# A hybrid decoder layer on one core: where the products of each group of heads stand, and which engine copies the state

## The chip, the cores and the metric

The kernel runs on one core of a Trainium2 chip. A core has a tensor engine (PE, matmuls and transposes; PEld is its weight load), a vector engine (DVE), a scalar engine (ACT), GpSimd (POOL) and a queue engine for transfers (SP). Each takes its instructions in a fixed order, and they wait for one another by semaphores. The metric is the time of one execution of the program on the device, in microseconds (us); of several runs the median is taken. One further execution is recorded by the hardware profiler; all durations below come from it.

## The reference

One decoder layer, `SEQ` 256, `D_MODEL` 2048, in float32:

```python
u = rmsnorm(h, norm_mix_pre)
z, xbc, dt_raw, q, k, v = split(u @ w_in)
xbc = silu(causal_depthwise_conv(xbc, conv_w, conv_b))     # width 4
xs, bm, cm = split(xbc)                                    # 8 groups of 4 heads, state 128
a_cs = cumsum(dt * a)                                      # chunks of 128: two of them
decay_in = exp(where(causal, a_cs[i] - a_cs[j], -inf))
y_diag = (cb * decay_in) @ xdt                             # within a chunk
states = bm^T (decay_to_end * xdt)                         # state at the end of a chunk
y_off = (cc @ previous_state) * exp(a_cs)                  # read-out of the earlier chunk
yg = (y_diag + y_off + d_skip * xh) * silu(z)
y_ssm = grouped_rmsnorm(yg) * ssm_norm_w
y_att = dilated_window_attention(q, k, v)                  # three dilations, mixed
h = h + rmsnorm(concat(y_ssm, y_att) @ w_out, norm_mix_post)
h = h + rmsnorm(relu(rmsnorm(h) @ w_up) ** 2 @ w_down, norm_mlp_post)
```

The change lies in the groups of heads: `y_diag`, `states` and `y_off` for each of the eight groups.

## The kernel before, in words

Most of the time goes to the large products with the weights `w_in`, `w_out`, `w_up` and `w_down` in columns of 512. Weights come from memory in blocks of two rows of 128 (`raw`, 512 KB). Each block is split in two: ScalarE writes the high part (`hi`, L147) and VectorE the rest (`lo`, L148). PE multiplies with both (L475 with `hi`, L478 with `lo` where a product has its features on the partitions; L328 to L330 and L411 to L413 where it has the positions there). A product over all 2048 rows is eight blocks, and a block of the first kind is eight L475 and eight L478. There are five buffers each for `hi` and `lo` and four for `raw`, so ScalarE's split of a later block waits until PE has finished with an earlier one.

The smaller work is written as Python generators, which are laid in between. A deque `waiting` holds them. After each block of weights `pump()` takes the first generator, runs it up to its next `yield` (one portion) and puts it at the deque's end. With two groups of heads in the deque, a group advances by one portion every second block. The groups come in pairs: two are queued after the conv of each set of x columns, and are laid into the blocks of the products that follow. In the trace these are the places near 140 to 160 us (groups 0 and 1), 186 to 207 us (2 and 3), 292 to 310 us (4 and 5) and 330 to 352 us (6 and 7). After groups 0 to 3 and 4 to 7 the gate columns and then further columns of `w_in` follow.

A group's generator (`ssd_group`) has these portions. First the cumulated decays are fetched into `bc` (L787). Then L793 to L811: C times B (`cbm`), B and x turned round by transposes, and on VectorE and GpSimd the scaled x (`xdt`, `xdd`, `xs`). Then the decays: `Relu` and `Exp` on ScalarE (L820, L821), times `cbm` on VectorE (L822); the state's product (L825, into one half of a small bank `ps`) and its copy `st` (L827). Then the read-out with the state (L829, into the other half of the same bank), its scaling by VectorE (`yo`, L831), its sum on GpSimd (L833), and eight products of the decays with `xdt` (L837) in a new bank. VectorE adds and gates (L840, L842), ScalarE squares (L846), VectorE and GpSimd work out the root (L141, L142), VectorE scales (L850). After two empty portions the result is turned round (L857) and split into `sh` and `sl` (L149, L150) for the product with `w_out`.

All small work shares two banks (`psmall`), which go round: a bank can be taken again when its last reader is done. `Exp` (L821) and `Silu` (L753, L776) need different tables in ScalarE; before a change of table an `ACT_TABLE_LOAD` stands in its order.

A scheduler sets the final order of instructions on each engine from the order in which they were written, from priorities (`tc.high_priority`; the weights' fetches and splits have the highest, `AHEAD`) and from what each depends on. So a moved portion can shift other instructions too.

Of the kernel before, what the change touches and what calls it, by code (L numbers as in the profile page):

```python
# [13 lines left out]
AF = mybir.ActivationFunctionType  # L14
# [3 lines left out]
S = 256  # L18
# [59 lines left out]
def hymba_layer(ctx: ExitStack, tc: tile.TileContext, x, norm_mix_pre, w_in, conv_w, conv_b, dt_bias, a_log,  # L78
                d_skip, ssm_norm_w, w_out, norm_mix_post, norm_mlp_pre, w_up, w_down, norm_mlp_post,
                consts, out):  # L80
    nc = tc.nc
# [53 lines left out]
    def psmall():  # L135
        return psm.tile([P, NB], F32, name="ps")

    def rsqrt_mean(dst, sums, n):

        m = cp.tile(list(sums.shape), F32, name="rm", bufs=2)  # L140
        nc.vector.tensor_scalar(m, sums, 1.0 / n, EPS, op0=ALU.mult, op1=ALU.add)  # L141
        nc.gpsimd.tensor_tensor(dst, m, half[:, :sums.shape[1]], op=ALU.pow)  # L142

    def split(hi, lo, src, scale=None):

        if scale is None:
            return (nc.scalar.activation(hi, src, AF.Copy),  # L147
                    nc.vector.tensor_tensor(lo, src, hi.bitcast(F32), op=ALU.subtract))  # L148
        return (nc.scalar.activation(hi, src, AF.Copy, scale=scale),  # L149
                nc.vector.scalar_tensor_tensor(lo, src, scale, hi.bitcast(F32), op0=ALU.mult, op1=ALU.subtract))  # L150
# [632 lines left out]
    def ssd_group(sp, g, bT, cT, xT, z):  # L783

        hs = slice(HPG * g, HPG * (g + 1))
        bc = sp.tile([P, HPG, S], F32, name="bc")
        nc.scalar.dma_start(bc, acs_d[hs].partition_broadcast(P))  # L787
        yield

        p = psmall()  # L790
        for c in range(NT):
            cs = slice(c * P, (c + 1) * P)
            nc.tensor.matmul(p[:, cs], bT[:, cs], cT[:, cs], start=True, stop=True)  # L793
        nc.tensor.transpose(p[:, S:S + P], bT[:, 0:P], ident)
        cbm = sp.tile([P, NT, P], F32, name="cbm")
        nc.vector.tensor_tensor(cbm, p[:, :S].rearrange("p (c i) -> p c i", c=NT),
                                triu[:, None, :].to_broadcast([P, NT, P]), op=ALU.mult)
        bn = sp.tile([P, P], F32, name="bn")
        nc.scalar.activation(bn, p[:, S:S + P], AF.Copy)

        p = psmall().rearrange("p (c f) -> p c f", c=NT)
        for c in range(NT):
            for f in range(2):
                nc.tensor.transpose(p[:, c, f * P:(f + 1) * P], xT[:, f, c * P:(c + 1) * P], ident)
        xs = sp.tile([P, NT, HPG, HD], F32, name="xs")
        nc.scalar.activation(xs.rearrange("p c r d -> p c (r d)"), p, AF.Copy)
        xdt = sp.tile([P, NT, HPG, HD], F32, name="xdt")
        for c in range(NT):
            nc.vector.tensor_tensor(xdt[:, c], xs[:, c], dt[:, c, hs, None].to_broadcast([P, HPG, HD]), op=ALU.mult)
        xdd = sp.tile([P, HPG, HD], F32, name="xdd")  # L810
        nc.gpsimd.tensor_tensor(xdd, xdt[:, 0], toend[:, hs, None].to_broadcast([P, HPG, HD]), op=ALU.mult)  # L811
        for c in range(NT):
            nc.gpsimd.tensor_tensor(xs[:, c], xs[:, c], skip_b[:, hs, None].to_broadcast([P, HPG, HD]), op=ALU.mult)
        yield

        for c in range(NT):
            m = bc[:, :, c * P:(c + 1) * P]
            for r in range(HPG):
                h = HPG * g + r
                nc.scalar.activation(m[:, r], m[:, r], AF.Relu, scale=-1.0, bias=acs[:, c, h:h + 1])  # L820
            nc.scalar.activation(m, m, AF.Exp, scale=-1.0)  # L821
            nc.vector.tensor_tensor(m, m, cbm[:, c, None, :].to_broadcast([P, HPG, P]), op=ALU.mult)  # L822

        p = psmall()
        nc.tensor.matmul(p[:, :S], bn, xdd.rearrange("p r d -> p (r d)"), start=True, stop=True)  # L825
        st = sp.tile([P, HPG * HD], F32, name="st")
        nc.vector.tensor_copy(st, p[:, :S])  # L827
        yield
        nc.tensor.matmul(p[:, S:], cT[:, P:], st, start=True, stop=True)  # L829
        yo = sp.tile([P, HPG, HD], F32, name="yo")  # L830
        nc.vector.tensor_tensor(yo, p[:, S:].rearrange("p (r d) -> p r d", r=HPG),  # L831
                                eacs[:, hs, None].to_broadcast([P, HPG, HD]), op=ALU.mult)
        nc.gpsimd.tensor_tensor(xs[:, 1], xs[:, 1], yo, op=ALU.add)  # L833
        p = psmall().rearrange("p (c r d) -> p c r d", c=NT, r=HPG)
        for c in range(NT):
            for r in range(HPG):
                nc.tensor.matmul(p[:, c, r], bc[:, r, c * P:(c + 1) * P], xdt[:, c, r], start=True, stop=True)  # L837

        yg = sp.tile([P, NT, HPG * HD], F32, name="yg")
        nc.vector.tensor_tensor(yg, p.rearrange("p c r d -> p c (r d)"), xs.rearrange("p c r d -> p c (r d)"),  # L840
                                op=ALU.add)
        nc.vector.tensor_tensor(yg, yg, z, op=ALU.mult)  # L842
        gs = sp.tile([P, NT], F32, name="gs")
        for c in range(NT):
            junk = sp.tile([P, HPG * HD], BF16, name="gj")
            nc.scalar.activation(junk, yg[:, c], AF.Square, accum_out=gs[:, c:c + 1])  # L846
        gr = sp.tile([P, NT], F32, name="gr")
        rsqrt_mean(gr, gs, HPG * HD)
        for c in range(NT):
            nc.vector.tensor_scalar(yg[:, c], yg[:, c], gr[:, c:c + 1], None, op0=ALU.mult)  # L850
        yield
        yield
        yield
        p = psmall().rearrange("p (f s) -> p f s", f=2)
        for f in range(2):
            for c in range(NT):
                nc.tensor.transpose(p[:, f, c * P:(c + 1) * P], yg[:, c, f * P:(f + 1) * P], ident)  # L857
        with tc.high_priority(offset=200):
            for f in range(2):
                k = 2 * g + f  # L860
                split(sh[:, k], sl[:, k], p[:, f], w_ssm[:, k:k + 1])
# [3 lines left out]
    for hb in range(2):  # L865
        bT = conv_block(COL_B + hb * NB, 16 + 4 * hb, first if hb == 0 else None)
        if hb == 0:
            waiting.append(steps())
        cT = conv_block(COL_C + hb * NB, 24 + 4 * hb)
        for xb in (2 * hb, 2 * hb + 1):  # L870
            xT = conv_block(COL_X + xb * NB, 4 * xb)
            if xb % 2 == 0:
                zs += gates(xb)
            for j in range(2):
                g = 2 * xb + j
                waiting.append(ssd_group(sp, g, bT[:, g % 4], cT[:, g % 4], xT[:, 2 * j:2 * j + 2],
                                         zs[xb][:, :, j * 256:(j + 1) * 256]))
# [623 lines left out]
```

## Time and profile before

| | us |
|---|---|
| median of three runs | 1458.86 (1458.23 to 1462.82) |
| the profiled execution's own time | 1459.04 |
| its span, first to last instruction | 1457.3 |
| PE busy in it | 1446.1 (99%) |
| weight loads of PE | 1219.4 (84%) |
| DVE busy | 1281.2 (88%) |
| ACT busy | 939.1 (64%) |
| POOL busy | 150.3 (10%) |

The granted clock of TensorE was 0.999 of full speed. A row of a timeline gives the start and the duration in us, the engine, the line, the operation with the tile it writes and those it reads, and in brackets the engine's idle time ahead of it with what ended it. A row that has `x8` stands for eight in a run, and its duration is that of the whole run. A row of groups gives the total busy time and the mean in ns, and behind the second bar the idle time ahead of them. A row of stretches gives for each engine the busy time and, in brackets, the number of instructions; then the clock, the share of the DMA engines and GB/s.

### The profile page before, as it was taken

To read this page: it belongs to the slowest core of one execution; us is meant where nothing else is said; L and a number is where in the kernel's file an instruction comes from. 1 tells how busy PE (TensorE), PEld (TensorE's weight loads), DVE (VectorE), ACT (ScalarE), POOL (GpSimd) and SP (SyncE) were. 2 spreads that over 40 slices of the span, in tenths; PEclk is the share of its full clock that TensorE was granted. 3 is DMA by queue.
4 is the path that set the end of the run, shared out by engine and by line. 5 is a ranking of instruction groups with operands and counts; after the bars stand their busy time and mean duration, and the time that the engine had idled before them with its cause. 6 is when DMAs were issued, how large, how long until landed. Compare 5 with 4: busy or idle time off the path is not lost.

```text
span 1457.3 us, 20381 instructions
## 1 busy us (share of the span) xinstructions
PE 1446.1 (99%) x7099; PEld 1219.4 (84%) x7099; DVE 1281.2 (88%) x1843; ACT 939.1 (64%) x1346; POOL 150.3 (10%) x226
## 2 busy tenths in 40 slices
PE   9999999999999999999999999999999999999998
PEld 8888888888888888888888888888888888888886
DVE  7799898888997686689878999999889999999997
ACT  7577779566666565556657677656464776765664
POOL 0202120121010010010100011011111111101000
PEclk9999999999999999999999999999999999999999
DMA  8978556856675486688876798678888888788854
GB/s 271 279 204 235 177 175 185 247 174 202 186 220 174 130 238 202 194 261 253 270 224 213 207 318 240 196 223 255 249 238 275 257 245 247 208 281 258 260 181 160
DMA packets 170201, 328.27 MB, mean 225 GB/s; under 512 B 15617, under 2 KB 18545, under 8 KB 170097
## 3 DMA queue, kind: packets, MB, share of 16 engines
q1 hardware_dynamic: 144592, 272.37, 58.6%
q0 software_dynamic: 17632, 40.91, 14.0%
q10 hardware_dynamic: 7872, 13.68, 2.7%
q8 instruction: 56, 0.92, 0.2%
q14 instruction: 49, 0.39, 0.1%
HBM read 322.67 MB, written 45.12 MB: 252 GB/s over the span
## 4 chain that ended last, share of the span: by engine, by line
PE 95%; DVE 3%; ACT 1%; issue 1%; POOL 0%; ACTq 0%; DVEq 0%
PE acc L475 13%; PE acc L328 11%; PE acc L330 11%; PE acc L329 11%; PE acc L478 7%; PE acc L412 6%; PE acc L413 6%; PE acc L411 6%; PE ps L330 3%; PE ps L328 3%; PE ps L329 3%; PE ps L412 3%; PE ps L413 2%; PE ps L411 2%; DVE lo L148 1%; PE ps L837 1%
## 5 line engine op out<-in xcount | busy, mean ns | idle before, releaser
L148 DVE TENSOR_TENSOR lo<-raw,hi 128x1024 fp32r<-128x1024 f32 (+1 forms) x392 | 476.8, 1221 | 86.0 <-ACT hi L147 82.7
L147 ACT ACTIVATE hi<-raw 128x1024 fp32r<-128x1024 f32 (+1 forms) x392 | 409.7, 1050 | 209.0 <-PE acc L330 70.6
L475 PE MATMUL acc<-ua,hi 128*128 128x512 f32 x600 | 162.5, 400 | 0.0
L475 PEld LDWEIGHTS acc<-ua,hi 128*128 128x128 f32 x600 | 105.5, 189 | 16.4
L147 ACT ACTIVATE hi<-e 128x1024 fp32r<-128x1024 f32 x64 | 68.1, 1064 | 69.1 <-DVE e L252 64.2
L478 PEld LDWEIGHTS acc<-ua,lo 128*128 128x128 f32 x600 | 88.2, 190 | 10.0
L478 PE MATMUL acc<-ua,lo 128*128 128x256 f32 x600 | 91.5, 282 | 0.0
L328 PE MATMUL acc<-hi,sh 128*128 128x512 f32 x224 | 88.4, 395 | 0.0
L330 PE MATMUL acc<-hi,sl 128*128 128x512 f32 x224 | 87.3, 390 | 0.0
L329 PE MATMUL acc<-lo,sh 128*128 128x512 f32 x224 | 87.2, 389 | 0.0
L328 PE MATMUL acc<-hi,ua 128*128 128x512 f32 x216 | 85.5, 396 | 0.0
L329 PE MATMUL acc<-lo,ua 128*128 128x512 f32 x216 | 84.2, 390 | 0.0
L330 PE MATMUL acc<-hi,ua 128*128 128x512 f32 x216 | 84.2, 390 | 0.0
L148 DVE TENSOR_TENSOR lo<-e,hi 128x1024 fp32r<-128x1024 f32 x64 | 78.0, 1219 | 0.0
L475 PE MATMUL acc<-uc,hi 128*128 128x512 f32 x240 | 69.9, 402 | 0.0
L412 PE MATMUL acc<-lo,ah 128*128 128x512 f32 x174 | 67.8, 390 | 0.0
L411 PE MATMUL acc<-hi,ah 128*128 128x512 f32 x174 | 67.8, 389 | 0.0
L413 PE MATMUL acc<-hi,al 128*128 128x512 f32 x174 | 67.7, 389 | 0.0
L148 DVE TENSOR_TENSOR lo<-ha,hi 128x1024 fp32r<-128x1024 f32 x43 | 52.3, 1221 | 5.9 <-ACT hi L147 5.7
L147 ACT ACTIVATE hi<-ha 128x1024 fp32r<-128x1024 f32 x43 | 45.1, 1056 | 16.2 <-PE acc L330 9.5
L147 ACT ACTIVATE hi<-r 128x512 fp32r<-128x512 f32 x64 | 40.1, 627 | 18.3 <-PE acc L330 7.0
L330 PE MATMUL acc<-hi,al 128*128 128x512 f32 x128 | 49.8, 389 | 0.0
(544 smaller groups left out, 3612.7 us busy)
## 6 DMA issues: line engine op xcount, KB each, us to landing
raw<-in_w_in_dram SPq DMA_DIRECT2D x161, 512.0 KB, 4.5
raw<-in_w_down_dram SPq DMA_DIRECT2D x72, 512.0 KB, 5.2
raw<-in_w_up_dram SPq DMA_DIRECT2D x65, 512.0 KB, 4.7
raw<-in_w_out_dram SPq DMA_DIRECT2D x38, 512.0 KB, 5.1
pair<-in_w_up_dram POOLq DMA_DIRECT2D x56, 256.0 KB, 5.0
raw<-pair SPq DMA_DIRECT2D x52, 256.0 KB, 4.2
pair<-in_w_down_dram POOLq DMA_DIRECT2D x50, 256.0 KB, 6.2
ha<-in_w_up_dram SPq DMA_DIRECT2D x20, 512.0 KB, 4.9
```

Of the source, the lines that this page charges most:

```text
L147: return (nc.scalar.activation(hi, src, AF.Copy), nc.vector.tensor_tensor(lo, src, hi.bitcast(F32), op=ALU.subtract))
L148: nc.vector.tensor_tensor(lo, src, hi.bitcast(F32), op=ALU.subtract))
L328: nc.tensor.matmul(dst, a_h[:, r, ts], hi[:, j], start=begin and j == 0, stop=False)
L329: nc.tensor.matmul(dst, a_h[:, r, ts], lo[:, j], start=False, stop=False)
L330: product[t] = nc.tensor.matmul(dst, a_l[:, r, ts], hi[:, j], start=False, stop=end and j == KB - 1)
L411: nc.tensor.matmul(dst, a_h, hi[:, j], start=own and first, stop=False)
L412: nc.tensor.matmul(dst, a_h, lo[:, j], start=False, stop=False)
L413: nc.tensor.matmul(dst, a_l, hi[:, j], start=False, stop=own and last)
L475: nc.tensor.matmul(acc[f], hi[:, j, f * P:(f + 1) * P], u(k0 + j), start=k0 + j == 0, stop=False, skip_group_check=True)
L478: nc.tensor.matmul(acc[f][:, 0], lo[:, j, f * P:(f + 1) * P], u(k0 + j)[:, 0], start=False, stop=k0 + j == NK - 1, skip_group_check=True)
L837: nc.tensor.matmul(p[:, c, r], bc[:, r, c * P:(c + 1) * P], xdt[:, c, r], start=True, stop=True)
```

## The change

Three edits in `ssd_group`. The copy of the state from its bank goes from VectorE to ScalarE. A `yield` is put between the read-out's part (up to L833) and the decays' products (before L837, now L838), so these become a portion of their own with what follows them (L840 to L850, now L841 to L851). One of the two empty portions ahead of the transposes is taken out (of three `yield`s in a row two are left), so the number of portions of a group stays the same.

```diff
         p = psmall()
         nc.tensor.matmul(p[:, :S], bn, xdd.rearrange("p r d -> p (r d)"), start=True, stop=True)
         st = sp.tile([P, HPG * HD], F32, name="st")
-        nc.vector.tensor_copy(st, p[:, :S])
+        nc.scalar.activation(st, p[:, :S], AF.Copy)
         yield
         nc.tensor.matmul(p[:, S:], cT[:, P:], st, start=True, stop=True)
         yo = sp.tile([P, HPG, HD], F32, name="yo")
         nc.vector.tensor_tensor(yo, p[:, S:].rearrange("p (r d) -> p r d", r=HPG),
                                 eacs[:, hs, None].to_broadcast([P, HPG, HD]), op=ALU.mult)
         nc.gpsimd.tensor_tensor(xs[:, 1], xs[:, 1], yo, op=ALU.add)
+        yield
         p = psmall().rearrange("p (c r d) -> p c r d", c=NT, r=HPG)
...
             nc.vector.tensor_scalar(yg[:, c], yg[:, c], gr[:, c:c + 1], None, op0=ALU.mult)
-        yield
         yield
         yield
         p = psmall().rearrange("p (f s) -> p f s", f=2)
```

How the order of the instructions moves is shown at three places. First PE at groups 0 and 1: `st` is the state, `xdt` the scaled x, `bc` the decays, `uc`, `ua`, `hi` and `lo` belong to the blocks of weights. Before:

```order
L829 MATMUL ps<-st,cT 128x256
L475 MATMUL acc<-uc,hi 128x512 x2
L478 MATMUL acc<-uc,lo 128x256 x2
L475 MATMUL acc<-uc,hi 128x512 x2
L478 MATMUL acc<-uc,lo 128x256 x2
L837 MATMUL ps<-xdt,bc 128x64 x8
L475 MATMUL acc<-uc,hi 128x512 x2
L478 MATMUL acc<-uc,lo 128x256 x2
L475 MATMUL acc<-uc,hi 128x512 x2
L478 MATMUL acc<-uc,lo 128x256 x2
L829 MATMUL ps<-st,cT 128x256
L837 MATMUL ps<-xdt,bc 128x64 x8
```

After, from the second L829 (group 1) on; the eight rows of weights between it and the first L829 (group 0) are the same, without L837 among them:

```order
L829 MATMUL ps<-st,cT 128x256
L475 MATMUL acc<-ua,hi 128x512 x2
L478 MATMUL acc<-ua,lo 128x256 x2
L475 MATMUL acc<-ua,hi 128x512 x2
L478 MATMUL acc<-ua,lo 128x256 x2
L475 MATMUL acc<-ua,hi 128x512 x2
L478 MATMUL acc<-ua,lo 128x256 x2
L475 MATMUL acc<-ua,hi 128x512 x2
L478 MATMUL acc<-ua,lo 128x256 x2
L838 MATMUL ps<-xdt,bc 128x64 x8
L475 MATMUL acc<-ua,hi 128x512 x8
L478 MATMUL acc<-ua,lo 128x256 x8
```

Group 0's products, which stood half a block after its read-out, now stand two blocks after it, and group 1's, which followed its read-out at once, also two (a further L838 x8 follows the last row).

Second, VectorE ahead of group 2's state, up to the first split `sl` (L150) of an earlier group's result out of its bank (`cbm` is C times B, `xdt` the scaled x, `cT` and `pad` are columns of the next x, `lo` a block of weights). Before, from behind the first `cbm` (L796) and the two L822 on:

```order
L499 TENSOR_TENSOR cT<-acc,cT 128x256
L148 TENSOR_TENSOR lo<-raw,hi 128x1024
L499 TENSOR_TENSOR cT<-acc,cT 128x256 x2
L809 TENSOR_TENSOR xdt<-xs,dt 128x256
L148 TENSOR_TENSOR lo<-raw,hi 128x1024
L499 TENSOR_TENSOR cT<-acc,cT 128x256
L809 TENSOR_TENSOR xdt<-xs,dt 128x256
L796 TENSOR_TENSOR cbm<-ps,cst 128x256
L809 TENSOR_TENSOR xdt<-xs,dt 128x256 x2
L744 TENSOR_TENSOR pad<-cT,rbc 128x2x256 x2
L148 TENSOR_TENSOR lo<-raw,hi 128x1024
L150 SCALAR_TENSOR_TENSOR sl<-ps,par,sh 128x256
```

After, from behind the first `cbm` on:

```order
L809 TENSOR_TENSOR xdt<-xs,dt 128x256
L499 TENSOR_TENSOR cT<-acc,cT 128x256
L809 TENSOR_TENSOR xdt<-xs,dt 128x256
L499 TENSOR_TENSOR cT<-acc,cT 128x256
L822 TENSOR_TENSOR bc<-bc,cbm 128x4x128
L499 TENSOR_TENSOR cT<-acc,cT 128x256 x2
L796 TENSOR_TENSOR cbm<-ps,cst 128x256
L148 TENSOR_TENSOR lo<-raw,hi 128x1024
L809 TENSOR_TENSOR xdt<-xs,dt 128x256 x2
L744 TENSOR_TENSOR pad<-cT,rbc 128x2x256 x2
L822 TENSOR_TENSOR bc<-bc,cbm 128x4x128
L148 TENSOR_TENSOR lo<-raw,hi 128x1024
```

The L150 follows there too. The same work stands in both but for the splits of weights: three L148 before, two now; the third has gone ahead of the first `cbm`. Behind this L150 stand two L751, one L148 and two more L150 before, and three L751, one L148 and two more L150 now.

Third, PE at groups 6 and 7, where L825 makes the state. Before, from group 7's L825 on:

```order
L825 MATMUL ps<-xdd,bn 128x256
L475 MATMUL acc<-ua,hi 128x512
L829 MATMUL ps<-st,cT 128x256
L475 MATMUL acc<-ua,hi 128x512 x7
L478 MATMUL acc<-ua,lo 128x256 x6
L829 MATMUL ps<-st,cT 128x256
L478 MATMUL acc<-ua,lo 128x256 x2
L475 MATMUL acc<-ua,hi 128x512 x8
L478 MATMUL acc<-ua,lo 128x256 x2
L837 MATMUL ps<-xdt,bc 128x64 x16
```

After, from group 6's read-out L829 on; its L825 stands five rows higher, with four L475 and four L478 in between:

```order
L829 MATMUL ps<-st,cT 128x256
L475 MATMUL acc<-ua,hi 128x512 x6
L825 MATMUL ps<-xdd,bn 128x256
L475 MATMUL acc<-ua,hi 128x512 x2
L478 MATMUL acc<-ua,lo 128x256 x8
L838 MATMUL ps<-xdt,bc 128x64 x8
L475 MATMUL acc<-ua,hi 128x512
L829 MATMUL ps<-st,cT 128x256
L475 MATMUL acc<-ua,hi 128x512 x7
L478 MATMUL acc<-ua,lo 128x256 x8
L838 MATMUL ps<-xdt,bc 128x64 x8
```

Both states were made before either was read; now group 6 is read first, and group 7's state is made after that. In the built program both states now go to the same one of the two small banks, so group 7's L825 comes behind group 6's L831. From the last products to the transposes L857 stood six L478 and two blocks, and now two blocks.

At the same place, ScalarE after the change (`cT` are copies of finished columns, `sh` the split of an earlier group's result, `bc` the decays, `hi` a block of weights):

```order
L820 ACTIVATE bc<-bc,acs 128x128 x2
L827 ACTIVATE st<-ps 128x256
L820 ACTIVATE bc<-bc,acs 128x128 x3
L147 ACTIVATE hi<-raw 128x1024
L149 ACTIVATE sh<-ps,par 128x256
L821 ACTIVATE bc<-bc 128x4x128
L820 ACTIVATE bc<-bc,acs 128x128 x3
L147 ACTIVATE hi<-raw 128x1024
L821 ACTIVATE bc<-bc 128x4x128
L827 ACTIVATE st<-ps 128x256
```

The two L827 are new in this order; the second stands behind a split and an `Exp`. The tables move as well: ScalarE has as many `ACT_TABLE_LOAD` as before, but two that stood ahead of groups 2 and 3 (for an `Exp`, L821, between two `Silu`, L753) now stand behind them, at the gate columns near 212 to 265 us.

## The prediction

> **What bounds the kernel now.** I read the page's totals first, then the chain that ended last, and then the waits of the tensor engine alone, since these say how much any change off that engine can give back.
>
> ```profile
> PE 1446.1 (99%) x7099; PEld 1219.4 (84%) x7099; DVE 1281.2 (88%) x1843; ACT 939.1 (64%) x1346; POOL 150.3 (10%) x226
> PE 95%; DVE 3%; ACT 1%; issue 1%; POOL 0%; ACTq 0%; DVEq 0%
> ```
>
> PE is the bound: busy 99% of the span, and 95% of the chain. The change alters no matmul, so what can be won is PE's idle time. The list of its waits has eight rows (what PE waited for; total, times, longest). Four are outside the groups of heads:
>
> ```profile
> PE ps L1353 <- ACT dg L1352: 1.7, 1, 1.7
> PE ps L526 <- DVE half L515: 1.1, 1, 1.1
> ...
> PE acc L1131 <- DVE ha L1122: 0.2, 1, 0.2
> PE ps L412 <- DVE lo L148: 0.2, 1, 0.2
> ```
>
> The other four lie in the code that the change touches. The timeline of PE gives their places and sizes:
>
> ```profile
> 150.76 1.44 PE L837 MATMUL ps<-xdt,bc 128*128 128x64 f32 x11 [0.73 <-DVE yo L831]
> ...
> 191.77 0.67 PE L825 MATMUL ps<-xdd,bn 128*128 128x256 f32 x2 [1.76 <-DVE sl L150]
> ...
> 198.63 0.70 PE L829 MATMUL ps<-st,cT 128*128 128x256 f32 x2 [0.17 <-DVE st L827]
> ...
> 321.79 0.86 PE L475 MATMUL acc<-ub,hi 128*128 128x512 f32 x3
> 323.13 0.71 PE L793 MATMUL ps<-cT 128*128 128x128 f32 x4 [0.49 <-ACT bn L799]
> ```
>
> 0.73 + 1.76 + 0.17 + 0.49 = 3.15 us, or 0.22% of the span. That is the ceiling of the gain, and it lies below 0.3% (4.4 us), which is about what a measurement of this kernel can tell from no change. A loss has no such ceiling. So the question is which of the four waits go, and which come in their place. I number the pairs of groups 1 to 4 (groups 0/1 near 140 to 160 us, 2/3 near 186 to 207, 4/5 near 292 to 310, 6/7 near 330 to 352).
>
> The profiled execution took 1459.04 us with a span of 1457.3; it stands 0.18 above the median of the runs, 1458.86.
>
> **The products get their own portion: pair 1.** Before, one portion holds the read-out L829, its scaling L831 on VectorE and the products L837. PE reaches L837 of group 0 while L831 is still queued on VectorE, and both tiles go through the same two small banks: that is the 0.73. Now two blocks of weights stand between the read-out and the products, where half a block or none stood (first place of the order above). A block takes about 2.8 us (the two L829 quoted under pair 4, at 336.37 and 339.18, have 7 of its 8 L475 and 6 of its 8 L478 between them). L831 was 0.73 late for L837, so with 1.5 blocks (4.2 us) more it is 3.5 early: gain 0.73. The other bank's user comes a block later too, and the number of portions up to the transposes is the same, so I put no new wait here; a bound for one is the same 0.73.
>
> **The copy on ScalarE: pairs 1 and 3.** What it takes away and what it adds, and the nearest prices:
>
> ```profile
> L827 DVE COPY st<-ps x8: 410/412/423, 146.8 to 338.7; 128x256 f32<-128x256 f32 x8
> ...
> L498 ACT ACTIVATE cT<-acc 128x256 f32<-128x256 f32 x56 | 21.0, 381 | 16.4 <-PE acc L478 16.2
> L147 ACT ACTIVATE hi<-raw 128x1024 fp32r<-128x1024 f32 (+1 forms) x392 | 409.7, 1050 | 209.0 <-PE acc L330 70.6 <-PE acc L475 49.3 <-issue 21.1
> ```
>
> VectorE loses 8 x 0.412 = 3.3 us over four pairs; ScalarE gains 8 x 0.38 = 3.0 us (L498 has the same shape, source and operation, so I take it). Neither is PE's time. In pair 1 the copy falls into ScalarE's idle time:
>
> ```profile
> 147.32 1.06 ACT L147 ACTIVATE hi<-raw 128x1024 fp32r<-128x1024 f32 x1 [2.16 <-PE acc L475]
> ```
>
> ```profile
> 144.80 0.59 PE L825 MATMUL ps<-xdd,bn 128*128 128x256 f32 x2
> ```
>
> ```profile
> 146.76 0.41 DVE L827 COPY st<-ps 128x256 f32<-128x256 f32 x1
> ...
> 148.83 0.41 DVE L827 COPY st<-ps 128x256 f32<-128x256 f32 x1
> ```
>
> ScalarE idles 2.16 us because it waits for PE to free a buffer. The matmul L825 of group 1 stands at 144.80, so its copy can be done by about 146, where VectorE began it only at 148.83. Cost nothing; the cover is the 2.16, and were it gone, the split behind the copy would be 0.38 late. Pair 3 had no wait of PE, and its copies stand between the same splits. Between 0 and 0.38 for each of the four I take 0.
>
> **Pair 2.** The 1.76 is a wait for a bank: L825 of group 2 needs the second half of the split L150 out of it. VectorE's rows up to there:
>
> ```profile
> 176.57 0.42 DVE L796 TENSOR_TENSOR cbm<-ps,cst 128x256 f32<-128x256 f32 x1 [0.63 <-PE ps L794]
> ...
> 178.12 0.69 DVE L822 TENSOR_TENSOR bc<-bc,cbm 128x512 f32<-128x512 f32 x1 [0.40 <-ACT bc L821]
> 179.34 0.42 DVE L499 TENSOR_TENSOR cT<-acc,cT 128x256 f32<-128x256 f32 x1 [0.53 <-ACT cT L498]
> ...
> 189.23 0.87 DVE L751 SCALAR_TENSOR_TENSOR cT<-pad,cw,cT 128x256 f32<-128x256 f32 x2
> 190.02 1.21 DVE L148 TENSOR_TENSOR lo<-raw,hi 128x1024 fp32r<-128x1024 f32 x1
> 191.15 0.86 DVE L150 SCALAR_TENSOR_TENSOR sl<-ps,par,sh 128x256 fp32r<-128x256 f32 x2
> ```
>
> The run starts at 176.57 on a PE event and has no idle after the 0.53. In the changed order (second place above) one lo split (1.22) less stands in that run and one L751 (0.43) more: 0.79 less. The two small idles, 0.40 and 0.53, are behind ScalarE, which now has two table loads fewer ahead of this place: up to 0.93 more. So L150 comes 0.79 to 1.72 earlier against PE, and 0.04 to 0.97 of the 1.76 is left. I take 0.3 left, since ScalarE loses 2 x 1.28 us of loads there (rows below), more than the 0.93: gain 1.46, between 0.79 and 1.72. Further on, the copies of groups 2 and 3 stand behind one table load with its SiLU on ScalarE and are due at L829, 6.9 us after L825 of the same group (191.77 and 198.63): the 0.17 goes.
>
> **The table loads that move.** The groups' loads are as many as before, but two come to stand in the stretch 212 to 265 us, where the gates' columns run:
>
> ```profile
> 176.16 1.28 ACT L821 ACT_TABLE_LOAD   x1
> 177.46 0.64 ACT L821 ACTIVATE bc<-bc 128x512 f32<-128x512 f32 x1
> ```
>
> ```profile
> 220.00:240.00 20.00, 20.00 (x114) 17.42 (x113) 15.89 (x26) 19.88 (x36) 1.57 (x3) 1.00 0.66 185
> ```
>
> ```profile
> 247.58 2.36 DVE L148 TENSOR_TENSOR lo<-raw,hi 128x1024 fp32r<-128x1024 f32 x2
> ```
>
> ```profile
> 250.60 0.39 PE L328 MATMUL acc<-hi,ua 128*128 128x512 f32 x1
> 250.83 0.39 PE L329 MATMUL acc<-lo,ua 128*128 128x512 f32 x1
> ```
>
> ScalarE is busy 19.88 of 20 us at 220 to 240. The first lo of the row at 247.58 ends at 248.80 and PE uses it at 250.83: a lead of 2.03, the least in this stretch. Two loads are 2.57 us, and the activation follows its load by 0.02. The two loads that went from ahead of pair 2 let ScalarE enter the stretch earlier, so I count about 1 us of lag and no wait; between 0 and 2.57 - 2.03 = 0.5 us lost I take 0, the nearer for a lag of 1. The Trainium skill ("ScalarE: Activation LUTs", section What ACT_TABLE_LOAD costs) gives 1283 ns for the load and some 1380 ns more for a drain, 2.66 us a switch. The trace has the same 1283 but no drain behind it; with the skill's figure the two loads would be an estimated 5.3 us.
>
> **Pair 4.** This is the pair whose order changes most (third place above). PE's rows before:
>
> ```profile
> 336.37 0.59 PE L829 MATMUL ps<-st,cT 128*128 128x256 f32 x2
> ...
> 339.18 0.70 PE L829 MATMUL ps<-st,cT 128*128 128x256 f32 x2
> ```
>
> Now L825 of group 6 is followed by half a block (1.4 us) and L829. From L825's start to L829's are some 1.9 us, and the copy needs 0.59 + 0.38 of them, so 0.9 is to spare. L825 of group 7 now uses group 6's bank and waits for L831 of group 6: 0.59 + 0.42 (the 128x256 rows of VectorE above) = 1.0, against six L475 of 0.23 and L829's own step, some 1.8. L829 of group 7 waits for a copy behind a split (1.05, which itself waits for PE to free a buffer) and an Exp (0.64), with group 6's products between: about even, I count 0.2. The transposes L857 of group 4 now stand some 0.7 us behind group 7's (L804), and need the bank that ScalarE's copy of those empties; that copy has twice L498's elements, so the wait is between nothing and 2 x 0.38, and I count 0.35. The wait of 0.49 at L793, for another copy on ScalarE, is shortened to about 0.3 by the rows that went from ahead of it. Net 0.19 - 0.35 - 0.2 = -0.36. Bounds: all four even and the 0.49 gone, +0.49; or the rival below.
>
> **Sum.** 0.73 + 1.46 + 0.17 - 0.36 = 2.0 us; 1459.04 - 2.0 = 1457.0 for the profiled kind of execution, 1456.9 against the median.
>
> **Rivals.** *Eaten later.* From 352 us VectorE runs without pause, and the lead falls to 0.49 us (the lo that ends at 392.86 is used at 393.35):
>
> ```profile
> 352.00:408.00 56.00, 56.00 (x266) 46.84 (x265) 55.66 (x81) 35.18 (x47) 2.83 (x4) 1.00 0.72 221
> ```
>
> ```profile
> 345.79 0.69 DVE L840 TENSOR_TENSOR yg<-ps,xs 128x512 f32<-128x512 f32 x1 [0.37 <-PE ps L837]
> ...
> 351.67 0.62 DVE L850 TENSOR_SCALAR yg<-yg,gr 128x256 f32<-128x256 f32 x2 [0.80 <-POOL gr L142]
> ...
> 391.64 1.22 DVE L148 TENSOR_TENSOR lo<-cT,hi 128x1024 fp32r<-128x1024 f32 x1
> ```
>
> ```profile
> 393.35 0.39 PE L412 MATMUL acc<-lo,ah 128*128 128x512 f32 x1
> ```
>
> Group 7's products now end a portion later, with the same transposes behind: L840, L842, the squares, GpSimd's root and L850 have two blocks and group 6's transposes, some 6.1 us, where they took 6.5 before (345.79 to 352.29) with a lo split of 1.22 among them. If the run starts 2.8 us later, PE waits 2.8 - 0.49 = 2.3 and the gain is gone: 1459.2. Against it: VectorE has less to do ahead (no copies).
>
> *Slower: the single bank of pair 4.* If a split, an Exp and a load (1.05 + 0.64 + 1.28 = 2.97) stand ahead of the copy when it is due, group 6 is 2.1 late (2.97 less 0.9), and group 7, which can't start L825 before L831, 3.0. With pair 2's gain lost too, 1459.04 - 0.9 + 5.1 = 1463.2 (1460.5 to 1466). It decides as soon as the copy starts more than 0.9 us late. For it: ScalarE is 18.47 of 20 us busy there; against it: the order puts only scalings L820 and not a split ahead of group 6's copy.
>
> ```profile
> 320.00:340.00 20.00, 19.51 (x120) 16.73 (x119) 19.13 (x34) 18.47 (x39) 4.64 (x6) 1.00 0.55 148
> ```
>
> *The table loads are paid in full.* ScalarE is full at 220 to 240, so if the lead of 2.03 is used up by its other moved rows, both loads reach PE: 1457.0 + 2.6 = 1459.6. Against it: the lead, and the loads that went from ahead. By the skill's drain the same place would cost an estimated 5.3 - 2.03 = 3.3 us, 1460.3; no run here has shown that drain so far.
>
> *Faster.* If PE's busy time held hidden waits, more than 3.15 us could come back. The Trainium skill ("Perfetto Trace Analysis", section Identifying the Most-Contended Engine) warns that matmul busy time is a bad measure and points to weight loads, here 84%. Against it: three L475 in 0.86 us at 321.79, the last of them 0.40 long, step by 0.23, as the rows at 250.60 and 250.83 do far from the groups; no wait hides in such rows. If half a block's 2.8 us were hidden on top of the ceiling: 1459.04 - 3.15 - 1.4 = 1454.5.
>
> **How the numbers follow.** Forecast 0.43 (1456.9, own range 1455.7 to 1458.2), eaten later 0.18, single bank 0.27 (0.14 of it over 1463.2), loads 0.07 (0.01 over), faster 0.05. So faster by over 0.3% (below 1454.5) 0.05, within 0.80, slower (over 1463.2) 0.15. The range 1455.6 to 1463.5 takes in the full ceiling of 3.15 us and the centres of all rivals but the last.
>
> **What would show it.** Right: no wait at L838, under 1 us at L825, no wait at L829 in pairs 1 to 3, copies of 0.38 us on ScalarE. Wrong: a row of PE near 250 us or 390 us waiting for a split, or L829 or L825 of pair 4 waiting over 1 us for ScalarE's copy or for L831.

## The result, and the profile after

The changed kernel takes 1456.30 us (median of 9 runs, 1455.61 to 1457.04), the kernel before 1459.70 us over 9 runs beside it (1458.23 to 1462.82). The medians differ by 3.4 us. The ratio over all runs is 0.9974, with a 95% interval of 0.9964 to 0.9984, which is 3.8 us less, between 2.3 and 5.2. The forecast was 1456.9, a gain of 2.0 against the first three runs' median of 1458.86. Both the profiled span (1457.3 to 1454.7) and the profiled execution's time (1459.04 to 1456.44) are 2.6 lower.

The page's totals after with the shares of the chain that ended last, and then the list of PE's waits (total, times, longest):

```profile
PE 1445.2 (99%) x7099; PEld 1218.5 (84%) x7099; DVE 1277.6 (88%) x1835; ACT 941.1 (65%) x1354; POOL 151.1 (10%) x226
PE 94%; DVE 3%; ACT 1%; DMA 1%; issue 1%; DVEq 0%; ACTq 0%
```

```profile
PE ps L1353 <- ACT dg L1352: 1.7, 1, 1.7
PE ps L526 <- DVE half L515: 1.1, 1, 1.1
PE ps L887 <- DVE mx L895: 0.7, 1, 0.7
PE ps L825 <- DVE sl L150: 0.6, 1, 0.6
PE acc L1131 <- DVE ha L1122: 0.2, 1, 0.2
PE ps L412 <- DVE lo L148: 0.2, 1, 0.2
```

Of the four waits in the groups' code only L825 is left, at 0.65 instead of 1.76; those at L837, L829 and L793 are gone from the list. A new one stands in the attention, L887. The timeline of PE shows group 1's read-out and the first products, the state's product of group 2 and its read-out, and the new wait:

```profile
150.98 0.59 PE L829 MATMUL ps<-st,cT 128*128 128x256 f32 x2
151.22 0.81 PE L475 MATMUL acc<-ua,hi 128*128 128x512 f32 x2
...
153.99 0.39 PE L478 MATMUL acc<-ua,lo 128*128 128x256 f32 x2
154.22 1.89 PE L838 MATMUL ps<-xdt,bc 128*128 128x64 f32 x16
...
189.35 0.67 PE L825 MATMUL ps<-xdd,bn 128*128 128x256 f32 x2 [0.65 <-DVE sl L150]
...
195.88 0.59 PE L829 MATMUL ps<-st,cT 128*128 128x256 f32 x2
...
550.11 0.49 PE L887 MATMUL ps<-cT 128*128 128x128 f32 x2 [0.68 <-DVE mx L895]
```

Where the time went can be followed by the matmuls with weights, which are 6378 in both traces and stand in the same order. The table gives, for each stretch between two of them, by how much the changed kernel got through it faster (minus) or slower than the one before. The traces of three of the versions below stand beside it.

| stretch (us, before) | changed | portion alone | copy alone | copy twice |
|---|---|---|---|---|
| up to 141 | -0.28 | +0.27 | -0.30 | +0.60 |
| pair 1, 141 to 175 | -1.00 | -1.00 | -0.73 | -0.99 |
| pair 2, 175 to 232 | -1.74 | -1.72 | +0.05 | -1.71 |
| gates, 232 to 291 | 0.00 | 0.00 | 0.00 | 0.00 |
| pair 3, 291 to 315 | -0.26 | -0.26 | -0.01 | -0.26 |
| pair 4, 315 to 353 | -0.44 | -0.46 | +0.11 | -0.45 |
| 353 to 421 | 0.00 | 0.00 | 0.00 | 0.00 |
| behind 421 | +1.12 | -0.08 | -0.02 | -0.05 |
| whole | -2.60 | -3.25 | -0.90 | -2.86 |

The first row is a difference between executions, since no instruction differs ahead of the groups. The groups give back 3.44 us. In this one execution 1.12 is lost again behind them, 0.94 of it at 550 us. There ScalarE had waited for a transfer of weights:

```profile
541.47 1.06 ACT L147 ACTIVATE hi<-raw 128x1024 fp32r<-128x1024 f32 x1 [4.77 <-DMA raw<-in_w_in_dram]
```

Before, the longest such idle time there was 2.65 us, and no wait of PE followed. The versions with the portion alone, the copy twice and the late copy, counted from 141 us, reach this place just as early against the kernel before and have no wait at L887 (idle times of 4.34 us at most ahead of it). So it most likely belongs to this execution's transfers and not to the change, though one trace of each version can't prove it. The 3.4 us between the medians agree with the 3.44 of the groups.

### The profile page after: what moved, and what is told of

It reads as the page before. It is cut to its first block, busy times and chain, and to the rows that moved or that the text cites. A ratio compares the mean times of both kernels' runs of the same rounds, so it can differ in the third digit from the quotient of the medians.

```text
span 1454.7 us, 20377 instructions
## 1 busy us (share of the span) xinstructions
PE 1445.2 (99%) x7099; PEld 1218.5 (84%) x7099; DVE 1277.6 (88%) x1835; ACT 941.1 (65%) x1354; POOL 151.1 (10%) x226
## 4 chain that ended last, share of the span: by engine, by line
PE 94%; DVE 3%; ACT 1%; DMA 1%; issue 1%; DVEq 0%; ACTq 0%
PE acc L475 14%; PE acc L328 11%; PE acc L330 11%; PE acc L329 11%; PE acc L478 7%; PE acc L412 6%; PE acc L413 6%; PE acc L411 6%; PE ps L329 3%; PE ps L328 3%; PE ps L330 3%; PE ps L412 2%; PE ps L413 2%; PE ps L411 2%; DVE lo L148 1%; PE ps L838 1%
## 5 line engine op out<-in xcount | busy, mean ns | idle before, releaser
L148 DVE TENSOR_TENSOR lo<-raw,hi 128x1024 fp32r<-128x1024 f32 (+1 forms) x392 | 474.8, 1217 | 95.0 <-ACT hi L147 91.0
L475 PE MATMUL acc<-ua,hi 128*128 128x512 f32 x600 | 163.9, 402 | 0.1
L475 PEld LDWEIGHTS acc<-ua,hi 128*128 128x128 f32 x600 | 105.8, 189 | 16.9 <-ACT hi L147 0.2
L478 PEld LDWEIGHTS acc<-ua,lo 128*128 128x128 f32 x600 | 87.9, 189 | 10.1
L478 PE MATMUL acc<-ua,lo 128*128 128x256 f32 x600 | 90.5, 281 | 0.0
L148 DVE TENSOR_TENSOR lo<-e,hi 128x1024 fp32r<-128x1024 f32 x64 | 78.0, 1218 | 0.0
L475 PE MATMUL acc<-uc,hi 128*128 128x512 f32 x240 | 69.6, 401 | 0.0
L148 DVE TENSOR_TENSOR lo<-ha,hi 128x1024 fp32r<-128x1024 f32 x43 | 52.4, 1220 | 6.0 <-ACT hi L147 5.7
```

The costliest lines, as they stand in the source:

```text
L475: nc.tensor.matmul(acc[f], hi[:, j, f * P:(f + 1) * P], u(k0 + j), start=k0 + j == 0, stop=False, skip_group_check=True)
L478: nc.tensor.matmul(acc[f][:, 0], lo[:, j, f * P:(f + 1) * P], u(k0 + j)[:, 0], start=False, stop=k0 + j == NK - 1, skip_group_check=True)
```

## The experiments

Each was compared with the kernel before on the same chip, in five rounds.

**The portion alone**, the copy back on VectorE.

```diff
-        nc.scalar.activation(st, p[:, :S], AF.Copy)
+        nc.vector.tensor_copy(st, p[:, :S])
```

> The portions as in the changed kernel, the state's copy back on VectorE. Theory A (the portion carries the gain, through the half block to two blocks that now lie between the read-out and the products): no wait of PE at the products, a wait of at most 1 us at L825 of group 2, small waits of 0.2 to 0.5 us at L829 for the copy; in all 0.3 to 1 us slower than the changed kernel, 1456.6 to 1457.3 us. Theory B (VectorE's relief by eight copies of 0.41 us carries it): at least half of the gain of 3.4 us is missing, 1458 to 1459.7 us, with a wait of over 1.2 us at L825 of group 2.

Measured: 1456.30 us against 1459.20, ratio 0.9978 (0.9969 to 0.9987). That is the whole gain, and the waits of PE are those of the changed kernel without L887:

```profile
PE ps L1353 <- ACT dg L1352: 1.7, 1, 1.7
PE ps L526 <- DVE half L515: 1.1, 1, 1.1
PE ps L825 <- DVE sl L150: 0.6, 1, 0.6
PE acc L1131 <- DVE ha L1122: 0.2, 1, 0.2
PE ps L412 <- DVE lo L148: 0.2, 1, 0.2
```

Theory A holds, and more than it said: the waits that were expected at L829 for VectorE's copy did not come back. Before, the copy came just too late (0.17 us at L829 of group 2). With the products in a later portion it is done in time on either engine. Theory B is out.

**The copy alone**, with the portions as before.

```diff
-        nc.vector.tensor_copy(st, p[:, :S])
+        nc.scalar.activation(st, p[:, :S], AF.Copy)
```

> The portions as before the change, only the copy on ScalarE. Theory A: the wait at L837 of group 0 stays, if shorter by the copies that no longer stand ahead of L831 on VectorE (0.73 to about 0.3 us), and the read-out directly ahead of the products stays; the wait of 1.76 us at L825 stays over 1 us; 1458 to 1459.5 us. Theory B: both waits go, 1456.3 to 1457 us.

Measured: 1458.84 us against 1459.20, ratio 0.9996 (0.9987 to 1.0005).

```profile
PE ps L825 <- DVE sl L150: 1.7, 1, 1.7
...
PE ps L793 <- ACT bn L799: 0.5, 1, 0.5
PE ps L837 <- DVE yo L831: 0.4, 1, 0.4
```

```profile
200.35 1.89 PE L837 MATMUL ps<-xdt,bc 128*128 128x64 f32 x15 [0.40 <-DVE yo L831]
```

The listed wait at the products is gone from group 0 (0.73 gained in pair 1), where 0.3 was expected to stay; by the rows themselves some 0.16 is left, since the products stand 0.39 behind the last two rows of weights (149.34 to 149.73) and 0.23 in the changed kernel. But a wait of the same kind, 0.40, has come at a product of pair 2, and the 1.76 at L825 is 1.71. So here the copy's engine decides at which group VectorE is late for the products, and the portion decides whether it is late at all.

**The copy twice.** The change with a second copy on ScalarE.

```diff
         nc.scalar.activation(st, p[:, :S], AF.Copy)
+        twice = sp.tile([P, HPG * HD], F32, name="st2")
+        nc.scalar.activation(twice, p[:, :S], AF.Copy)
```

> The changed kernel with a second copy of the state on ScalarE into a tile that nothing reads (eight copies of 0.38 us more). If ScalarE's copies lie in its idle time, as the prediction has it: within 0.7 us of the changed kernel, no wait of PE over 0.5 us at L829 or its follower. If they don't, as the rival of the single bank has it: 0.4 us and more for each group of pairs 2 and 4, so 1.5 us and more slower than the changed kernel.

Measured: 1456.14 us against 1459.20, ratio 0.9979 (0.9970 to 0.9988), and the same gains in every pair (table above). ScalarE's copies lie beside other work.

**The copy late.** Three copies that nothing reads stand ahead of the one that is read.

```diff
+        for _ in range(3):
+            junk = sp.tile([P, HPG * HD], F32, name="st2")
+            nc.scalar.activation(junk, p[:, :S], AF.Copy)
         nc.scalar.activation(st, p[:, :S], AF.Copy)
```

> The changed kernel with three copies of the bank into a tile that nothing reads, on ScalarE ahead of the state's copy: it comes 0.85 to 1.1 us later. The prediction gave the copy of group 6 some 0.9 us to spare: then PE waits 0 to 0.3 us at L829 of group 6 and not in pairs 1 to 3, and the time is within 1 us of the changed kernel. If less is to spare: 0.5 us and more at L829 of groups 6 and 7, also of 2 and 3, in all 1.5 us and more slower.

Measured: 1456.29 us against 1459.61, ratio 0.9977 (0.9968 to 0.9986). The time is the one expected in the first case, with no wait listed for the copy. ScalarE's copies in pair 4 (L829 the junk, L830 the one that is read), and PE's read-outs, now L832:

```profile
331.88 0.94 ACT L829 ACTIVATE st<-ps 128x256 f32<-128x256 f32 x3
332.69 0.41 ACT L830 ACTIVATE st<-ps 128x256 f32<-128x256 f32 x1
...
338.90 0.38 ACT L830 ACTIVATE st<-ps 128x256 f32<-128x256 f32 x1
```

```profile
331.17 0.67 PE L825 MATMUL ps<-xdd,bn 128*128 128x256 f32 x2
333.31 0.59 PE L832 MATMUL ps<-st,cT 128*128 128x256 f32 x2
...
340.41 0.59 PE L832 MATMUL ps<-st,cT 128*128 128x256 f32 x2
```

The copy of group 6 ends at 333.10, having started 0.81 behind the first junk copy, and its read-out starts at 333.31. But the edit also moved PE's rows: the read-out now stands one L475 further behind its L825 (2.14 us from start to start, 1.91 in the changed kernel), so this run alone does not measure the margin. The changed kernel's own rows do:

```profile
330.90 0.38 ACT L827 ACTIVATE st<-ps 128x256 f32<-128x256 f32 x1
...
336.50 0.36 ACT L827 ACTIVATE st<-ps 128x256 f32<-128x256 f32 x1
```

```profile
330.19 0.67 PE L825 MATMUL ps<-xdd,bn 128*128 128x256 f32 x2
...
332.10 0.59 PE L829 MATMUL ps<-st,cT 128*128 128x256 f32 x2
...
337.79 0.59 PE L829 MATMUL ps<-st,cT 128*128 128x256 f32 x2
```

Group 6's copy ends at 331.28 with 0.82 us to spare (0.9 was counted), and group 7's at 336.86 with 0.93. So the copy on ScalarE costs nothing at the single bank of pair 4.

**The empty portion put back.** The change without its third edit: a group has one portion more.

```diff
         yield
         yield
+        yield
         p = psmall().rearrange("p (f s) -> p f s", f=2)
```

> The changed kernel with the removed empty portion put back: the products' portion is then one more, and a group's transposes come one portion later. If only the products' place counts: within 0.7 us of the changed kernel, 1455.6 to 1457.0. If the removal counts: the transposes of groups 0 and 1 now stand behind the state's product of groups 2 and 3, so the wait of 0.65 us at L825 goes, but VectorE's unbroken stretch behind group 7 starts a portion later and PE waits there, as it did with the state's portion (1.5 us at 403 us): 1457 to 1459.

Measured: 1463.54 us against 1459.61, ratio 1.0026 (1.0016 to 1.0035): 3.9 us slower than before, some 7 slower than the change.

```profile
PE acc L411 <- ACT hi L147: 4.0, 3, 2.2
...
PE ps L329 <- DVE lo L148: 1.5, 1, 1.5
```

Up to 353 us this version is ahead of the kernel before (by 4.8 us, measured from 141). Then it loses 8.7 us between 353 and 421, where the changed kernel loses nothing. Some 0.8 of both figures is only the last eight transposes, which now lie behind 353. The expectation had the right place and less than half the size. The first late row is a transfer of weights. When the last group is done, the kernel closes the groups' buffers and opens those of the next stage (`ah`, `al`) in the room that this frees. The last transposes, the issue of the first transfer into `ah`, and ScalarE's split of it, in the changed kernel and then in this version:

```profile
348.16 1.04 PE L857 MATMUL ps<-ident,yg 128*128 128x128 f32 x8
...
349.34 0.88 SPq L161 DMA_DIRECT2D ah<-in_w_in_dram  x2
...
357.38 1.06 ACT L147 ACTIVATE hi<-ah 128x1024 fp32r<-128x1024 f32 x1
```

```profile
357.46 0.60 PE L858 MATMUL ps<-ident,yg 128*128 128x128 f32 x4
...
358.14 0.88 SPq L161 DMA_DIRECT2D ah<-in_w_in_dram  x2
...
363.43 1.06 ACT L147 ACTIVATE hi<-ah 128x1024 fp32r<-128x1024 f32 x1 [3.12 <-DMA ah<-in_w_in_dram]
```

In all ten traces of this case that transfer is issued 0.07 to 0.17 us behind the end of the last transpose. Here both come 8.8 to 8.9 us later than in the changed kernel, though PE reaches 353 within 0.4 us of the time there. So ScalarE waits 3.12 us for the weights, VectorE then for ScalarE (2.78), and PE in turn for ScalarE's splits (1.45 at 373.26, 2.16 at 379.21).

**The state's product in a portion of its own too**, with one empty portion less for it.

```diff
+        yield
         p = psmall()
         nc.tensor.matmul(p[:, :S], bn, xdd.rearrange("p r d -> p (r d)"), start=True, stop=True)
...
         yield
-        yield
         p = psmall().rearrange("p (f s) -> p f s", f=2)
```

> The changed kernel with the state's product and copy in a portion of their own too, and the last empty portion but one taken out for it. If the wait left at L825 of group 2 (0.65 us) is only that this product comes too early for its bank: it goes, and the time is 0.5 to 0.8 us shorter, 1455.5 to 1455.8 us. Rival: with one portion less ahead of the transposes, the transposes of a group wait for VectorE's scaling, 1 us or more in each pair: 1458 to 1461 us.

Measured: 1459.46 us against 1459.20, ratio 1.0001 (0.9993 to 1.0010).

```profile
...
PE ps L329 <- DVE lo L148: 1.5, 1, 1.5
PE ps L857 <- DVE yg L852: 1.1, 2, 0.6
```

The wait at L825 is gone, as expected, but two transposes wait for VectorE's scaling, 0.60 and 0.51, and 3.9 us are lost between 353 and 421, the wait of 0.51 among them. The products of groups 6 and 7 stand a portion later while the transposes keep their place, and PE waits for a split on VectorE at 403 us (1.47): this is what the rival called eaten later described. How the rest of the 3.9 comes about was not taken apart.

**The transposes earlier**, for groups 0, 1, 4 and 5, and then for all.

```diff
         yield
-        yield
+        if g % 4 >= 2:
+            yield
         p = psmall().rearrange("p (f s) -> p f s", f=2)
```

> The changed kernel with one empty portion less for groups 0, 1, 4 and 5 alone, so that their transposes and splits come a portion earlier and are done before the next pair's L825. If the wait left at L825 of group 2 is the bank that L150 holds: it goes, with 0.65 us and some 0.16 more, and the rest stays: 1455.2 to 1455.8 us. Rival: the transposes then wait for VectorE's scaling L851, or the next pair's order shifts: no gain or up to 2 us slower, 1456 to 1458.

Measured: 1459.54 us against 1459.61, ratio 0.9999 (0.9991 to 1.0008).

```profile
...
PE ps L825 <- POOL xdd L811: 1.4, 2, 1.1
...
PE ps L858 <- DVE yg L851: 1.0, 2, 0.5
PE ps L838 <- PE acc L478: 0.7, 1, 0.7
```

L825 of group 2 no longer waits, so that wait was the bank that L150 holds. But 0.73 come at a product of pair 2, two transposes wait for VectorE's scaling (0.53 and 0.50), and the states of pair 4 now wait for GpSimd's `xdd` (1.14 and 0.29). Pair 4 is 2.65 us slower than before the change, not 0.44 faster, so both things that the rival named came, and the time lies above both expected ranges. Why `xdd` is late there was not taken apart.

```diff
         yield
-        yield
         p = psmall().rearrange("p (f s) -> p f s", f=2)
```

> The same for all groups. In the second pair of each set the transposes then stand about one block and a half behind the products, while the chain from the products over sums, squares and root to the scaling takes some 5 us without a split in it. If that chain counts, PE waits at L856 of groups 2, 3, 6 and 7, 0.5 to 2.5 us each: 1457 to 1461 us. If it is hidden: as the version for groups 0, 1, 4 and 5 alone, 1455.2 to 1455.8.

Measured: 1460.13 us against 1459.61, ratio 1.0003 (0.9995 to 1.0012). The time lies in the range expected if the chain counts, but the chain from the products to the scaling shows only as three waits of 0.5 us at most (1.3 in all); most of the rest is the loss above, at L825 (1.4) and L838 (0.7). So neither a portion more nor a portion less ahead of the transposes is as good as the two that the change leaves.

## Why the prediction was right

*What bounds.* PE's idle time gave the order of the size: 3.15 us listed, 2.0 forecast, 3.44 measured in the groups. But it was not the ceiling that the prediction called it: only 2.45 us of the listed waits went, and some 1 us came from time that the list does not hold (last section). Nor was some 4.4 us needed to be told from no change, as the prediction had it: with 3.4 us the interval ends at 0.9984, short of 1.

*Luck.* The time lies 0.6 us from the forecast, while the gain was 1.4 us larger than forecast. The two fit only because the forecast counts from 1458.86, the median of three runs, and the nine runs gave 1459.70.

*Pairs 1 and 3.* Pair 1: 0.73 forecast, 1.00 measured. The wait went, with some time beside it that no bracket had shown (last section). Pair 3: nothing forecast, since it had no listed wait, and 0.26 measured, also time without a bracket.

*The copy on ScalarE.* Costed at nothing, and it was nothing: alone 0.36 us between medians, within its interval, doubled and delayed without loss. But the 0.17 at L829 was booked to it, and it goes with the portion alone too.

*Pair 2.* L825 was to keep 0.3 of 1.76 and kept 0.65, inside the bounds of 0.04 and 0.97. VectorE's rows after:

```profile
175.15 1.23 DVE L148 TENSOR_TENSOR lo<-raw,hi 128x1024 fp32r<-128x1024 f32 x1 [1.74 <-ACT hi L147]
176.29 0.42 DVE L796 TENSOR_TENSOR cbm<-ps,cst 128x256 f32<-128x256 f32 x1
...
187.60 1.21 DVE L148 TENSOR_TENSOR lo<-raw,hi 128x1024 fp32r<-128x1024 f32 x1
188.74 0.86 DVE L150 SCALAR_TENSOR_TENSOR sl<-ps,par,sh 128x256 fp32r<-128x256 f32 x2
```

The run from L796 to this L150 shrank from 14.58 us (176.57 to 191.15) to 12.45, more than the 1.72 that was the upper bound. What the working missed is the run's start: it moved by 0.28 us and not by PE's 1.28, since VectorE was held by a split of weights that ScalarE delivered late (the 1.74). The stretch as a whole gave 1.74 us, against 1.46 + 0.17.

*The table loads.* No PE wait between 232 and 291 us, 0.00 in the table. The load and its activation after the change, in the same kind of place:

```profile
169.27 1.28 ACT L821 ACT_TABLE_LOAD   x1
170.57 0.63 ACT L821 ACTIVATE bc<-bc 128x512 f32<-128x512 f32 x1
```

They follow one another by 0.02 us here too. The Trainium skill ("ScalarE: Activation LUTs", section What ACT_TABLE_LOAD costs) adds a drain of some 1380 ns to each; no run here shows one. In all ten traces the activation starts at most 0.02 us behind its load, save one in each of the two versions with early transposes, which waits 1.18 us for VectorE.

*Pair 4.* This is the term that was wrong: -0.36 forecast, +0.44 measured. The transposes L857 of group 4 wait 0.05 by the profile and some 0.2 by the step to them (0.45 from 323.84 to 324.29, where 0.23 is usual), where 0.35 was counted. L829 of group 7, put at "about even" and 0.2, has its copy 0.93 us ahead and shows no listed wait. And the 0.49 at L793 went from the list whole, where 0.3 was to stay. The margin of 0.9 us at group 6's read-out, on which the slower rival hung, held: it was 0.82.

*The rivals.* Eaten later did not come with the change. Its third edit keeps the transposes at their portion: the first transfer into `ah` is issued at 349.34, 3.72 us earlier than before (353.06), as much as PE itself is ahead there. A loss behind 353 comes when the count or the balance is moved by one portion, and it is more than the 2.3 us given: 8.7 us between 353 and 421 when the transposes are late, by way of the transfer, which the prediction did not have, and 3.9 us when the products are. The faster rival had a true core: PE's busy time fell by 0.9 us with the same matmuls.

## What to carry to other kernels

Where a small chain of PE, VectorE and PE is laid between large matmuls, put a PE step that waits for another engine into a portion of its own, a block or more behind the step whose result it needs; which engine makes the small copy in between matters less, as long as it has idle time there. This does not hold for every step: here a portion for the state's product too lost the whole gain. Keep the distance to the chain's consumer when adding a portion: take an empty one out, because the stage behind may have no slack at all, and ask which transfers start only when the chain's buffers come free. And measure the single edits of a change: here the portions carried everything and the copy nothing that could be measured.

## What was not expected of the hardware

A wait of PE is larger than the idle time that the timeline prints, and small ones don't appear. Before, the last row of weights ahead of L837 of group 0, and the read-out of group 1 directly ahead of its products, in PE's timeline:

```profile
149.64 0.40 PE L478 MATMUL acc<-uc,lo 128*128 128x256 f32 x2
...
154.04 0.60 PE L829 MATMUL ps<-st,cT 128*128 128x256 f32 x2
```

From 149.64 to L837 at 150.76 are 1.12 us with a printed wait of 0.73; after the change the same two rows stand 0.23 apart (153.99 and 154.22). So the wait was 0.89: the bracket counts from the modelled end of the matmul before, and the next would have started 0.16 ahead of that end. And L829 to the products that follow (154.04 to 154.48) are 0.44 us with no bracket at all, where L829 to a block of weights is 0.24 (150.98 and 151.22). This second step is the same, to 0.01, in all five places of the kernel before and of the copy alone where products follow a read-out directly, so it looks like a cost of that succession and not like a wait; this was not tested.

Steps of these two kinds are the likeliest source of the difference between the 2.45 us of listed waits that went (3.15 less the 0.65 and 0.05 left) and the 3.44 us gained. Pair 3 shows both: group 4's products stood 0.39 behind the rows of weights ahead of them (300.45 to 300.84), and group 5's 0.43 behind their read-out (304.14 to 304.57). The warning of the Trainium skill ("Perfetto Trace Analysis", section Identifying the Most-Contended Engine) that the busy time of matmuls is no good measure of the distance to the limit agrees with that: 1446.1 to 1445.2 us busy for the same 7099 matmuls.

Fewer table loads did not make a faster kernel: the version with the empty portion put back has 14 of them in its whole trace instead of 20 and is the slowest of all, at 1463.54 us.
